# Two attentions on one core: third key tile padded from 16 to 128 rows, three score products in one PSUM bank

## The chip, the cores and the metric

The kernel runs on one core of a Trainium2 chip. The metric is device time in microseconds (us) of one execution; lower is better. The engines named here are PE (TensorE, matrix products; PEld is its weight load), DVE (VectorE), ACT (ScalarE), POOL (GpSimd) and SP (the queue that starts the loads from HBM).

## What is computed

The reference chains two transformer blocks over 256 tokens with 16 meta tokens in front (width 1024, float32). The first block (convolution mixers and a layer of 16384 small experts) is not touched by the change. The second block runs two attentions side by side on the normed input, eight heads each:

```
def stick_breaking_block(q, k, v, qpos, kpos):
    z = einsum('bhqd,bhkd->bhqk', q, k) * (SB_HEAD_DIM ** -0.5)
    causal = kpos[None, :] < qpos[:, None]
    u = where(causal, log_sigmoid(-z), 0.0)
    rest = cumsum(u, axis=3, reverse=True) - u
    a = where(causal, exp(log_sigmoid(z) + rest), 0.0)
    return einsum('bhqk,bhkd->bhqd', a, v)

def diff_attn_block(q, k, v, lam, slopes, qpos, kpos, qcid, kcid):
    s = einsum('bhcqd,bhckd->bhcqk', q, k) * (DF_HEAD_DIM ** -0.5)
    s = where(kcid <= qcid, s - slopes * abs(qpos - kpos), -inf)
    p = softmax(s)
    w = p[:, :, 0] - lam * p[:, :, 1]
    return einsum('bhqk,bhkd->bhqd', w, v)
```

The keys are 272 (16 + 256), so over tiles of 128 they are two whole tiles and one of 16. The queries are the 256 tokens.

## The kernel before, in words

Weights come in units of 128x1024 float32: SP loads a unit (`load_to`, L124), ACT and DVE split it into a rounded part and a rest (`split_to`, L145; the split is made two units ahead), and PE multiplies rounded and rest parts in `mm_w` (L164 to 171): 24 matmuls for each unit, with 256 or 272 columns moving. PE's and SP's order is the order of the program text; the order of ACT, DVE and POOL is set by a scheduler.

In the second block each head of an attention takes three units (query, key and value projections, `feat`, L871). Between the units PE does the small products of the heads that are under way; each head is a Python generator (`stick`, L892; `diff`, L930), and `advance` (L996) lets every running head do its next piece after each unit.

A stick-breaking head does this, with keys on the partitions and queries along the columns. For each of the three key tiles (`KT`, L839: 128, 128 and 16 keys; the queries that can see them are 256, 144 and 16, `Q0`, L840) it makes a product z of key and query (L897), each in a PSUM bank of its own (`at_tile`, L73, four banks in turn). DVE adds the causal mask (L899), ACT and DVE form the softplus e (L901 to 904). Two pieces later, PE sums e along the keys by products with a triangle or with ones (L917, product S, six of them, two or four touching the 16 rows), DVE subtracts (L918), ACT exponentiates (L919). Two pieces later the value product po (L924) adds up over the three tiles. `value` (L883) transposes the values by PE before that (pv_sv, pv_dv). A differential head makes its scores with 64 rows of key and query (ds, L941), turns the weights by PE transposes (pw, L963) and multiplies them by the values (dpo, L972: for the first 128 queries one tile of 128 keys and one of 16, for the second two of 128 and one of 16).

These small products are plain float32, of which PE runs each matmul as two instructions ("passes" in the following), with a weight load for each; transposes are one pass. The trace writes a matmul's weights as rows*columns: `16*128` is a weight tile of 16 rows and 128 columns.

The lines that the change touches are these:

```
839     KT = [(0, P), (P, P), (2 * P, NM)]
...
897             nc.tensor.matmul(pz[:kn, :n], k[:, k0:k0 + kn], q[:, Q0[kt]:], start=True, stop=True)
...
917                 nc.tensor.matmul(ps[:kn, Q0[j] - Q0[kt]:n], w[:jn, :kn], sps[j][:jn], start=(j == kt), stop=(j == 2))
...
924             nc.tensor.matmul(po[:, Q0[kt]:T], vt[:kn, kt, :], zs[kt][:kn], start=(kt == 0), stop=(kt == 2))
...
963                 nc.tensor.transpose(pw[:n, i * P:(i + 1) * P], ws[t][:, k0:k0 + n], ident)
...
972                 nc.tensor.matmul(po[:, :P], wT[:n, i, :], vt[:n, i, :], start=(i == 0), stop=(i == tl[-1][0]))
```

Of the kernel before, what the change touches and what calls it, by code (L numbers as in the profile page):

```python
# [8 lines left out]
F32 = mybir.dt.float32  # L9
# [41 lines left out]
def two_blocks(ctx, tc, x, feats, vecs, w_in, w_out, w_q, keys, u, v, final_g, meta2, w_in2, lams, w_gate,  # L51
# [787 lines left out]
    KT = [(0, P), (P, P), (2 * P, NM)]  # L839
    Q0 = [0, 112, 240]  # L840
    QS = slice(NM, L)
# [7 lines left out]
    mneg = []  # L849
    for kt, (k0, kn) in enumerate(KT):  # L850
        m = psb.tile([P, T - Q0[kt]], F32, tag=f"mneg{kt}", name=f"mneg{kt}")
        nc.gpsimd.memset(m, 0.0)
        nc.gpsimd.affine_select(m[:kn], m[:kn], [[1, T - Q0[kt]]], ALU.is_gt, -BIG, base=NM + Q0[kt] - k0,
                                channel_multiplier=-1)
        mneg.append(m)
# [15 lines left out]
    def feat(name, tag, cols, scale=1.0):  # L871
        width = cols.stop - cols.start
        ps = mm_tile(f"ps_{name}")
        mm_w(ps[:, :width], xT2, cols)

        def scaled():
            o = psb.tile([P, width], F32, tag=tag, name=name, bufs=2)
            nc.vector.scalar_tensor_tensor(o, ps[:, :width], scale, rsb[:, cols], op0=ALU.mult, op1=ALU.mult)
            return o

        return scaled

    def value(name, tag, vt):  # L883
        ps = at_tile(f"pv_{name}")
        o = psb.tile([P, 3, P], F32, tag=tag, name=name, bufs=2)
        for kt, (k0, kn) in enumerate(KT):
            nc.tensor.transpose(ps[:kn, kt * P:(kt + 1) * P], vt[:, k0:k0 + kn], ident)
        nc.scalar.activation(o[:, :2, :], ps[:, :2 * P].rearrange("p (a b) -> p a b", a=2), AF.Copy)
        nc.scalar.activation(o[:NM, 2, :], ps[:NM, 2 * P:3 * P], AF.Copy)
        return o  # L890

    def stick(hd, q, k, vT):  # L892
        zs, sps = [], []
        for kt, (k0, kn) in enumerate(KT):
            n = T - Q0[kt]
            pz = at_tile(f"z{hd}{kt}")
            nc.tensor.matmul(pz[:kn, :n], k[:, k0:k0 + kn], q[:, Q0[kt]:], start=True, stop=True)  # L897
            z = psb.tile([P, n], F32, tag=f"z{kt}", name=f"zs{hd}{kt}", bufs=2)
            nc.vector.tensor_tensor(z[:kn], pz[:kn, :n], mneg[kt][:kn], op=ALU.add)  # L899
            e = psb.tile([P, n], F32, tag=f"e{kt}", name=f"e{hd}{kt}", bufs=2)  # L900
            nc.scalar.activation(e[:kn], z[:kn], AF.Abs)  # L901
            nc.scalar.activation(e[:kn], e[:kn], AF.Exp, scale=-1.0)
            nc.scalar.activation(e[:kn], e[:kn], AF.Ln, bias=1.0)
            nc.vector.scalar_tensor_tensor(e[:kn], z[:kn], 0.0, e[:kn], op0=ALU.max, op1=ALU.add)
            zs.append(z)
            sps.append(e)
# [4 lines left out]
        for kt, (k0, kn) in enumerate(KT):  # L911
            n = T - Q0[kt]
            ps = at_tile(f"S{hd}{kt}")
            for j in range(kt, 3):
                jn = KT[j][1]
                w = tri if j == kt else ones
                nc.tensor.matmul(ps[:kn, Q0[j] - Q0[kt]:n], w[:jn, :kn], sps[j][:jn], start=(j == kt), stop=(j == 2))  # L917
            nc.vector.tensor_tensor(zs[kt][:kn], zs[kt][:kn], ps[:kn, :n], op=ALU.subtract)  # L918
            nc.scalar.activation(zs[kt][:kn], zs[kt][:kn], AF.Exp)  # L919
# [3 lines left out]
        for kt, (k0, kn) in enumerate(KT):  # L923
            nc.tensor.matmul(po[:, Q0[kt]:T], vt[:kn, kt, :], zs[kt][:kn], start=(kt == 0), stop=(kt == 2))  # L924
# [5 lines left out]
    def diff(hd, q, k, vT):  # L930
        slope = 2.0 ** (-(hd + 1))
        ws = []
        for t in range(2):
# [15 lines left out]
            nc.vector.scalar_tensor_tensor(pe[0], pe[0], sm[:, 0:1], pe[1], op0=ALU.mult, op1=ALU.subtract)  # L949
            ws.append(pe[0])  # L950
# [6 lines left out]
        for t in range(2):  # L957
            kn = KN[t]
            pw = at_tile(f"pw{hd}{t}")
            wT = psb.tile([P, 3, P], F32, tag="wT", name=f"wT{hd}{t}", bufs=2)  # L960
            tl = [(i, k0, min(n, kn - k0)) for i, (k0, n) in enumerate(KT) if k0 < kn]
            for i, k0, n in tl:
                nc.tensor.transpose(pw[:n, i * P:(i + 1) * P], ws[t][:, k0:k0 + n], ident)  # L963
            f = len(tl) - 1
            nc.scalar.activation(wT[:, :f, :], pw[:, :f * P].rearrange("p (a b) -> p a b", a=f), AF.Copy)
            nc.scalar.activation(wT[:NM, f, :], pw[:NM, f * P:(f + 1) * P], AF.Copy)
            outs.append((wT, tl))
        yield
        for t, (wT, tl) in enumerate(outs):
            po = at_tile(f"dpo{hd}{t}")  # L970
            for i, k0, n in tl:
                nc.tensor.matmul(po[:, :P], wT[:n, i, :], vt[:n, i, :], start=(i == 0), stop=(i == tl[-1][0]))  # L972
            nc.scalar.activation(od[t][:, hd, :], po[:, :P], AF.Copy)
# [27 lines left out]
    for hd in range(NH):  # L1001
        q = feat(f"sq{hd}", "sq", QS, float(P) ** -0.5)
# [3 lines left out]
        k = feat(f"sk{hd}", "sk", FULL)  # L1006
# [6 lines left out]
        vT = feat(f"svT{hd}", "vT", FULL)  # L1013
# [11 lines left out]
    for hd in range(NH):  # L1025
        q = feat(f"dq{hd}", "dq", QS, 0.125)()
        advance()
        k = feat(f"dk{hd}", "dk", FULL)()
        advance()
        vT = feat(f"dvT{hd}", "vT", FULL)()  # L1030
# [162 lines left out]
```

## Time and profile before

| | before |
|---|---|
| time, median of 3 runs (us) | 1479.19 (1478.61, 1479.19, 1486.41) |
| time of the profiled execution (us) | 1478.11 |
| its span, first to last instruction (us) | 1476.4 |
| mean granted TensorE clock | 0.997 |
| busy: PE, PEld, DVE, ACT, POOL (us) | 1446.7, 1338.5, 1059.0, 746.6, 14.1 |
| DMA, mean (GB/s) | 169 |

Starts and durations below are us from the start of the span. A matmul's recorded duration overlaps that of its neighbours, so what a matmul costs is read from the distance between starts, not from the duration. The two attentions stand between about 950 and 1177 us: stick-breaking heads to about 1070, differential heads after.

### The profile page before, as it was taken

The page shows a single profiled execution, that of the slowest core. Times are in us where ns is not written, and L with a number is a line of the kernel's source. Part 1 is how long each engine was busy: PE and PEld are TensorE (multiplying, and loading weights), DVE is VectorE, ACT ScalarE, POOL GpSimd, SP SyncE. Part 2 cuts the span into 40 slices and gives each one's busy share as a digit, 9 for nine tenths or more (in the row PEclk, how much of TensorE's full clock was granted, in tenths as well). Part 3 has the DMA queues.
Part 4 walks back from the last instruction along what each step waited for, and adds up shares of the span by engine and source line. Part 5 has one row for each costly group of instructions (what it writes and reads, how often), then busy time and mean ns, then how long its engine had stood idle before and what let it go on. Part 6 is the DMA issues. An engine that isn't in the chain of part 4 may idle for free.

```text
span 1476.4 us, 25739 instructions
## 1 busy us (share of the span) xinstructions
PE 1446.7 (98%) x10096; PEld 1338.5 (91%) x10096; DVE 1059.0 (72%) x1936; ACT 746.6 (51%) x1312; POOL 14.1 (1%) x32
## 2 busy tenths in 40 slices
PE   8999999999999999999999999999999999999998
PEld 7988999999999999788888888889998999899997
DVE  8987669779788999655555565755577776766665
ACT  7556444445444443344444445655455674554444
POOL 0010000000000000000000000100000000000000
PEclk9999999999999999999999999999999999999999
DMA  7626666665544444466666676633334456556662
GB/s 236 199 72 201 197 177 193 189 184 186 168 140 143 143 144 129 141 192 195 188 196 196 191 252 190 190 125 115 127 115 130 128 171 184 165 186 194 187 187 98
DMA packets 69816, 248.96 MB, mean 169 GB/s; under 512 B 7744, under 2 KB 9152, under 8 KB 69696
## 3 DMA queue, kind: packets, MB, share of 16 engines
q1 hardware_dynamic: 68544, 243.13, 52.9%
q0 software_dynamic: 1152, 4.19, 0.8%
q8 instruction: 79, 1.29, 0.4%
q14 instruction: 41, 0.34, 0.1%
HBM read 245.20 MB, written 2.10 MB: 168 GB/s over the span
## 4 chain that ended last, share of the span: by engine, by line
PE 93%; DVE 5%; issue 1%; DMA 0%; ACT 0%; SPq 0%; DVEq 0%; ACTq 0%
PE v L184 8%; PE v L182 8%; PE v L183 8%; PE u L171 7%; PE u L169 7%; PE u L170 7%; PE gp L675 4%; PE fg L170 1%; PE fu L171 1%; PE fg L171 1%; PE fu L170 1%; PE fd L184 1%; PE fu L169 1%; PE fg L169 1%; PE fd L183 1%; PE fd L182 1%
## 5 line engine op out<-in xcount | busy, mean ns | idle before, releaser
L152 DVE TENSOR_TENSOR lo<-raw,hi 128x1024 fp32r<-128x1024 f32 x453 | 552.9, 1223 | 241.4 <-ACT hi L150 239.9
L150 ACT ACTIVATE hi<-raw 128x1024 fp32r<-128x1024 f32 x453 | 478.6, 1058 | 469.7 <-PE u L170 122.7
L169 PE MATMUL u<-hThi,hi 128*128 128x256 f32 x1024 | 289.9, 283 | 0.0
L171 PE MATMUL u<-hThi,lo 128*128 128x256 f32 x1024 | 285.3, 279 | 0.1
L170 PE MATMUL u<-hTlo,hi 128*128 128x256 f32 x1024 | 284.9, 278 | 0.0
L182 PE MATMUL v<-hi,w_hi 128*128 128x512 f32 x512 | 199.3, 389 | 1.3 <-ACT w_hi L764 1.3
L184 PE MATMUL v<-hi,w_lo 128*128 128x512 f32 x512 | 199.3, 389 | 0.5 <-DVE w_lo L766 0.5
L183 PE MATMUL v<-lo,w_hi 128*128 128x512 f32 x512 | 199.2, 389 | 0.0
L170 PEld LDWEIGHTS u<-hTlo,hi 128*128 128x128 f32 x1024 | 194.0, 189 | 0.0
L171 PEld LDWEIGHTS u<-hThi,lo 128*128 128x128 f32 x1024 | 192.3, 188 | 0.8 <-DVE lo L152 0.7
L169 PEld LDWEIGHTS u<-hThi,hi 128*128 128x128 f32 x1024 | 192.5, 188 | 0.0
L182 PEld LDWEIGHTS v<-hi,w_hi 128*128 128x128 f32 x512 | 96.1, 188 | 21.4 <-ACT w_hi L764 1.5
L184 PEld LDWEIGHTS v<-hi,w_lo 128*128 128x128 f32 x512 | 96.1, 188 | 20.9 <-DVE w_lo L766 1.0
L183 PEld LDWEIGHTS v<-lo,w_hi 128*128 128x128 f32 x512 | 96.1, 188 | 20.1 <-DVE lo L152 0.2
L675 PE MATMUL gp<-ga,gb 128*128 128x128 f32 x512 | 66.6, 275 | 4.0 <-DVE gb L666 4.0
L764 ACT ACTIVATE w_hi<-ewa 128x512 fp32r<-128x512 f32 x48 | 30.2, 632 | 76.7 <-PE v L183 65.9
L675 PEld LDWEIGHTS gp<-ga,gb 128*128 128x128 f32 x512 | 61.7, 191 | 4.8 <-PE gp L675 3.6
L766 DVE TENSOR_TENSOR w_lo<-ewa,w_hi 128x512 fp32r<-128x512 f32 x48 | 33.2, 693 | 38.6 <-ACT w_hi L764 38.6
L662 DVE TENSOR_TENSOR ga<-o,o 128x512 f32<-128x512 f32 x64 | 44.0, 687 | 17.8 <-PE gp L675 17.3
L170 PE MATMUL fg<-hTlo,hi 128*128 128x256 f32 x176 | 49.2, 280 | 0.5 <-DVE hTlo L223 0.5
L169 PE MATMUL fg<-hThi,hi 128*128 128x256 f32 x176 | 49.3, 280 | 0.3 <-ACT hThi L222 0.3
L171 PE MATMUL fu<-hThi,lo 128*128 128x256 f32 x176 | 49.1, 279 | 0.0
(403 smaller groups left out, 2970.6 us busy)
## 6 DMA issues: line engine op xcount, KB each, us to landing
raw<-in_u_dram SPq DMA_DIRECT2D x128, 512.0 KB, 3.6
raw<-in_v_dram SPq DMA_DIRECT2D x128, 512.0 KB, 3.6
raw<-in_w_in_dram SPq DMA_DIRECT2D x67, 512.0 KB, 3.6
raw<-in_w_fg_dram SPq DMA_DIRECT2D x22, 512.0 KB, 3.6
raw<-in_w_fu_dram SPq DMA_DIRECT2D x22, 512.0 KB, 3.6
raw<-in_w_fd_dram SPq DMA_DIRECT2D x22, 512.0 KB, 3.6
raw<-in_w_out_dram SPq DMA_DIRECT2D x16, 512.0 KB, 3.6
raw<-in_w_q_dram SPq DMA_DIRECT2D x16, 512.0 KB, 4.3
```

The costliest lines, as they stand in the source:

```text
L150: latest["hi"] = nc.scalar.activation(hi, loaded[i], AF.Copy)
L152: latest["lo"] = nc.vector.tensor_tensor(lo, loaded[i], hi.bitcast(F32), op=ALU.subtract)
L169: nc.tensor.matmul(ps, hi[:, ks], ahi[:, k, cols], start=(k == 0), stop=False)
L170: nc.tensor.matmul(ps, hi[:, ks], alo[:, k, cols], start=False, stop=False)
L171: nc.tensor.matmul(ps, lo[:, ks], ahi[:, k, cols], start=False, stop=(k == KC - 1))
L182: nc.tensor.matmul(ps, ahi[:, ts], hi[:, bs], start=first and n == 0, stop=False)
L183: nc.tensor.matmul(ps, ahi[:, ts], lo[:, bs], start=False, stop=False)
L184: nc.tensor.matmul(ps, alo[:, ts], hi[:, bs], start=False, stop=end)
L662: nc.vector.tensor_tensor(a.rearrange("p t (h l) -> p t h l", h=8), o8[:, tl, :].unsqueeze(3).broadcast_to((P, 4, 8, TOPK)), o16[:, tl, :] ...
L675: nc.tensor.matmul(p3[:, :, i], b[:, i, :], a[:, i, :], start=True, stop=True)
L764: nc.scalar.activation(hi, a, AF.Copy)
L766: nc.vector.tensor_tensor(lo, a, hi.bitcast(F32), op=ALU.subtract)
```

## The change: padding, one bank, and fewer instructions off PE

The key and value tiles become 384 columns wide and the differential weights 256 and 384, with zeros in the columns past the 272 keys (or past 144 for the first 128 queries); the zeros are written once by POOL into buffers that stay (two for the keys, one for the values, one for each of the two weight tiles). Every product over the third key tile then has 128 rows and 128 weight columns. The three z of a stick-breaking head stand side by side in one bank (256 + 144 + 16 = 416 columns), and so do its three S; DVE and ACT handle them with one instruction of 416 columns in place of three.

```
-    KT = [(0, P), (P, P), (2 * P, NM)]
+    KP = 3 * P
     Q0 = [0, 112, 240]
+    QN = [T - q0 for q0 in Q0]
+    QO = [0, QN[0], QN[0] + QN[1]]
+    NQ = sum(QN)
...
+    KW = [2 * P, KP]
+    padded = {}
+    for tag, n, w in (("k", L, KP), ("vT", L, KP), ("w0", KN[0], KW[0]), ("w1", KN[1], KW[1])):
+        padded[tag] = [psb.tile([P, w], F32, tag=f"{tag}{i}", name=f"{tag}pad{i}")
+                       for i in range(2 if tag == "k" else 1)]
+        for o in padded[tag]:
+            nc.gpsimd.memset(o[:, n:], 0.0)
...
+    def qcols(kt, j=None):
+        j = kt if j is None else j
+        return slice(QO[kt] + Q0[j] - Q0[kt], QO[kt] + QN[kt])
+
     def stick(hd, q, k, vT):
...
+        pz = at_tile(f"z{hd}")
+        for kt in range(3):
+            nc.tensor.matmul(pz[:, qcols(kt)], k[:, kt * P:(kt + 1) * P], q[:, Q0[kt]:], start=True, stop=True)
+        z = psb.tile([P, NQ], F32, tag="z", name=f"zs{hd}", bufs=2)
+        nc.vector.tensor_tensor(z, pz[:, :NQ], mneg, op=ALU.add)
+        e = psb.tile([P, NQ], F32, tag="e", name=f"e{hd}", bufs=2)
+        nc.scalar.activation(e, z, AF.Abs)
+        nc.scalar.activation(e, e, AF.Exp, scale=-1.0)
+        nc.scalar.activation(e, e, AF.Ln, bias=1.0)
+        nc.vector.scalar_tensor_tensor(e, z, 0.0, e, op0=ALU.max, op1=ALU.add)
...
+        ps = at_tile(f"S{hd}")
+        for kt in range(3):
             for j in range(kt, 3):
...
+                nc.tensor.matmul(ps[:, qcols(kt, j)], tri if j == kt else ones, e[:, qcols(j)],
+                                 start=(j == kt), stop=(j == 2))
+        nc.vector.tensor_tensor(z, z, ps[:, :NQ], op=ALU.subtract)
+        nc.scalar.activation(z, z, AF.Exp)
...
+        for kt in range(3):
+            nc.tensor.matmul(po[:, Q0[kt]:T], vt[:, kt, :], z[:, qcols(kt)], start=(kt == 0), stop=(kt == 2))
...
+            for i in range(nk):
+                nc.tensor.transpose(pw[:, i * P:(i + 1) * P], ws[t][:, i * P:(i + 1) * P], ident)
...
+            for i in range(nk):
+                nc.tensor.matmul(po[:, :P], wT[:, i, :], vt[:, i, :], start=(i == 0), stop=(i == nk - 1))
```

PE, the pieces S and z between two projections of a stick-breaking head, before (tiles are out<-in; the last number pair is the output's rows x columns):

```order
L917 MATMUL S_10796<-e_10661,tri 128x256
L917 MATMUL S_10796<-e_10670,ones 128x144
L917 MATMUL S_10796<-e_10679,ones 128x16
L917 MATMUL S_10802<-e_10670,tri 128x144
L917 MATMUL S_10802<-e_10679,ones 128x16
L917 MATMUL S_10807<-e_10679,tri 16x16
L897 MATMUL z_10811<-sq_10715,sk_10755 128x256
L897 MATMUL z_10820<-sq_10715,sk_10755 128x144
L897 MATMUL z_10829<-sq_10715,sk_10755 16x16
```

The same place in the change:

```order
L924 MATMUL S_10706<-e_10592,tri 128x256
L924 MATMUL S_10706<-e_10592,ones 128x144
L924 MATMUL S_10706<-e_10592,ones 128x16
L924 MATMUL S_10706<-e_10592,tri 128x144
L924 MATMUL S_10706<-e_10592,ones 128x16
L924 MATMUL S_10706<-e_10592,tri 128x16
L909 MATMUL z_10715<-sq_10628,kpad_10049 128x256
L909 MATMUL z_10715<-sq_10628,kpad_10049 128x144
L909 MATMUL z_10715<-sq_10628,kpad_10049 128x16
```

Nothing moved and the count is the same; the outputs of 16 rows became 128 rows, and S and z are one tile each.

DVE, from the value projection's scaling to the next query's, before (lo is the rest part of a weight unit, zs the masked z, e the softplus):

```order
L878 SCALAR_TENSOR_TENSOR svT_10794<-ps_svT_10763,rsb 128x272
L918 TENSOR_TENSOR zs_10659<-zs_10659,S_10796 128x256
L918 TENSOR_TENSOR zs_10668<-zs_10668,S_10802 128x144
L918 TENSOR_TENSOR zs_10677<-zs_10677,S_10807 16x16
L899 TENSOR_TENSOR zs_10813<-z_10811,mneg_10032 128x256
L899 TENSOR_TENSOR zs_10822<-z_10820,mneg_10037 128x144
L899 TENSOR_TENSOR zs_10831<-z_10829,mneg_10042 16x16
L152 TENSOR_TENSOR lo_10843<-raw_10725,hi_10841 128x1024
L904 SCALAR_TENSOR_TENSOR e_10815<-zs_10813,e_10815 128x256
L904 SCALAR_TENSOR_TENSOR e_10824<-zs_10822,e_10824 128x144
L904 SCALAR_TENSOR_TENSOR e_10833<-zs_10831,e_10833 16x16
```

The same place in the change:

```order
L889 SCALAR_TENSOR_TENSOR vTpad_10053<-ps_svT_10674,rsb 128x272
L152 TENSOR_TENSOR lo_10731<-raw_10637,hi_10729 128x1024
L926 TENSOR_TENSOR zs_10590<-zs_10590,S_10706 128x416
L911 TENSOR_TENSOR zs_10719<-z_10715,mneg 128x416
L889 SCALAR_TENSOR_TENSOR sq_10757<-ps_sq_10726,rsb 128x256
L916 SCALAR_TENSOR_TENSOR e_10721<-zs_10719,e_10721 128x416
```

Nine instructions became three, the weight split lo now stands ahead of the two that wait for S and z, and the next query's scaling (sq) ahead of the last step of e.

## Rows read from the trace of the kernel before

**Rows 1.** The page: PE's busy time and the chain that ended last, by engine.

```profile
PE 1446.7 (98%) x10096; PEld 1338.5 (91%) x10096; DVE 1059.0 (72%) x1936; ACT 746.6 (51%) x1312; POOL 14.1 (1%) x32
...
PE 93%; DVE 5%; issue 1%; DMA 0%; ACT 0%; SPq 0%; DVEq 0%; ACTq 0%
```

**Rows 2.** Busy time in the stretch of one differential head: length, PE, PEld, DVE, ACT, POOL.

```profile
1108.30:1121.20 12.90, 12.90 (x100) 11.64 (x98) 9.19 (x21) 6.93 (x20) 0.00 (x0) 1.00 0.41 123
```

**Rows 3.** PE in order of time, S and z of a stick-breaking head: start, us, instructions.

```profile
1000.54 0.59 PE L917 MATMUL S<-e,tri 128*128 128x256 f32 x2
...
1002.07 0.39 PE L917 MATMUL S<-e,ones 16*128 16x16 f32 x2
...
1002.53 1.09 PE L897 MATMUL z<-sq,sk 128*128 128x256 f32 x6
1003.55 0.39 PE L169 MATMUL ps_sq<-xT2hi,hi 128*128 128x256 f32 x1
1003.78 0.28 PE L170 MATMUL ps_sq<-xT2lo,hi 128*128 128x256 f32 x1
1003.90 0.28 PE L171 MATMUL ps_sq<-xT2hi,lo 128*128 128x256 f32 x1
```

**Rows 4.** PE in order of time, po of a stick-breaking head.

```profile
996.32 1.16 PE L924 MATMUL po<-zs,sv 128*128 128x256 f32 x6
997.41 0.40 PE L169 MATMUL ps_svT<-xT2hi,hi 128*128 128x272 f32 x1
```

**Rows 5.** PE in order of time, dpo of a differential head, whole and piece by piece.

```profile
1137.49 1.85 PE L972 MATMUL dpo<-dv,wT 128*128 128x128 f32 x10
1139.27 0.50 PE L941 MATMUL ds<-dk,dq 64*128 64x272 f32 x2
...
1137.80 0.48 PE L972 MATMUL dpo<-dv,wT 16*128 16x128 f32 x2
...
1138.22 0.38 PE L972 MATMUL dpo<-dv,wT 128*128 128x128 f32 x1
```

**Rows 6.** PE in order of time: eight float32 passes of full weights, 128 columns moving.

```profile
162.06 1.06 PE L539 MATMUL sc<-kt,qT 128*128 128x128 f32 x8
162.87 0.37 PE L169 MATMUL u<-hThi,hi 128*128 128x256 f32 x1
163.07 0.28 PE L170 MATMUL u<-hTlo,hi 128*128 128x256 f32 x1
```

**Rows 7.** PE in order of time: full weights with 16 columns moving, then 256 columns.

```profile
89.35 0.29 PE L250 MATMUL m_s<-m_q,ones 128*128 128x16 f32 x2
89.49 0.48 PE L182 MATMUL wo<-hi,yhi 128*128 128x512 f32 x1
89.81 0.39 PE L183 MATMUL wo<-lo,yhi 128*128 128x512 f32 x1
90.04 0.40 PE L184 MATMUL wo<-hi,ylo 128*128 128x512 f32 x1
...
98.19 0.59 PE L425 MATMUL ln_var<-csq,inv 128*128 128x256 f32 x2
98.62 0.50 PE L463 MATMUL pss<-ones,ysq 128*128 128x1 f32 x4
```

**Rows 8.** PE in order of time: the three value transposes, the third of 16 weight columns.

```profile
1006.49 0.49 PE L887 MATMUL pv_sv<-ident,svT 128*128 128x128 f32 x3
1006.73 0.38 PE L169 MATMUL ps_sk<-xT2hi,hi 128*128 128x272 f32 x1
1006.95 0.29 PE L170 MATMUL ps_sk<-xT2lo,hi 128*128 128x272 f32 x1
```

**Rows 9.** DVE's last step of e, and the S product that reads it.

```profile
1006.03 0.16 DVE L904 SCALAR_TENSOR_TENSOR e<-zs,e 16x16 f32<-16x16 f32 x1 [0.17 <-ACT e L903]
...
1014.07 0.38 PE L917 MATMUL S<-e,tri 128*128 128x256 f32 x1
```

**Rows 10.** Busy time by stretch ahead of the first head; the seventh field is PEclk.

```profile
962.70:966.20 3.50, 3.50 (x19) 3.50 (x19) 0.86 (x3) 1.03 (x2) 0.00 (x0) 0.51 0.44 174
```

More of the change, by code (lines that the diff above doesn't have):

```diff
@@ L846, in two_blocks @@
     s_sb, psb = phase("psb")
[L849 to L855, printed above, removed]
+    mneg = psb.tile([P, NQ], F32, tag="mneg", name="mneg")
+    nc.gpsimd.memset(mneg, 0.0)
+    for kt in range(3):
+        o = mneg[:, QO[kt]:QO[kt] + QN[kt]]
+        nc.gpsimd.affine_select(o, o, [[1, QN[kt]]], ALU.is_gt, -BIG, base=NM + Q0[kt] - kt * P, channel_multiplier=-1)
     tri = psb.tile([P, P], F32, tag="tri", name="tri")
@@ L876, in scaled @@
         def scaled():
-            o = psb.tile([P, width], F32, tag=tag, name=name, bufs=2)
-            nc.vector.scalar_tensor_tensor(o, ps[:, :width], scale, rsb[:, cols], op0=ALU.mult, op1=ALU.mult)
+            o = padded[tag][hd % len(padded[tag])] if tag in padded else psb.tile([P, width], F32, tag=tag, name=name, bufs=2)
+            nc.vector.scalar_tensor_tensor(o[:, :width], ps[:, :width], scale, rsb[:, cols], op0=ALU.mult, op1=ALU.mult)
             return o
@@ L885, in value @@
         o = psb.tile([P, 3, P], F32, tag=tag, name=name, bufs=2)
[L886 to L889, printed above, removed]
-        return o
+        for kt in range(3):
+            nc.tensor.transpose(ps[:, kt * P:(kt + 1) * P], vt[:, kt * P:(kt + 1) * P], ident)
+        nc.scalar.activation(o, ps[:, :KP].rearrange("p (a b) -> p a b", a=3), AF.Copy)
+        return o
+    def qcols(kt, j=None):
+        j = kt if j is None else j
+        return slice(QO[kt] + Q0[j] - Q0[kt], QO[kt] + QN[kt])
     def stick(hd, q, k, vT):
[L893 to L906, printed above, removed]
+        pz = at_tile(f"z{hd}")
[8 more added lines that the diff above has]
+        nc.vector.scalar_tensor_tensor(e, z, 0.0, e, op0=ALU.max, op1=ALU.add)
         yield
@@ L910, in stick @@
         yield
-        for kt, (k0, kn) in enumerate(KT):
-            n = T - Q0[kt]
-            ps = at_tile(f"S{hd}{kt}")
+        ps = at_tile(f"S{hd}")
+        for kt in range(3):
             for j in range(kt, 3):
[L915 to L919, printed above, removed]
+                nc.tensor.matmul(ps[:, qcols(kt, j)], tri if j == kt else ones, e[:, qcols(j)],
+                                 start=(j == kt), stop=(j == 2))
+        nc.vector.tensor_tensor(z, z, ps[:, :NQ], op=ALU.subtract)
+        nc.scalar.activation(z, z, AF.Exp)
         yield
@@ L922, in stick @@
         po = at_tile(f"po{hd}")
-        for kt, (k0, kn) in enumerate(KT):
-            nc.tensor.matmul(po[:, Q0[kt]:T], vt[:kn, kt, :], zs[kt][:kn], start=(kt == 0), stop=(kt == 2))
+        for kt in range(3):
+            nc.tensor.matmul(po[:, Q0[kt]:T], vt[:, kt, :], z[:, qcols(kt)], start=(kt == 0), stop=(kt == 2))
         nc.scalar.activation(osb[0][:, hd, :], po[:, :T], AF.Copy)
@@ L948, in diff @@
             nc.vector.tensor_scalar(pe[1], pe[1], sm[:, 1:2], lam, op0=ALU.mult, op1=ALU.mult)
-            nc.vector.scalar_tensor_tensor(pe[0], pe[0], sm[:, 0:1], pe[1], op0=ALU.mult, op1=ALU.subtract)
-            ws.append(pe[0])
+            w = padded[f"w{t}"][0]
+            nc.vector.scalar_tensor_tensor(w[:, :kn], pe[0], sm[:, 0:1], pe[1], op0=ALU.mult, op1=ALU.subtract)
+            ws.append(w)
             if t == 0:
@@ L1025, in two_blocks @@
     for hd in range(NH):
-        q = feat(f"dq{hd}", "dq", QS, 0.125)()
+        q = feat(f"dq{hd}", hd, "dq", QS, 0.125)()
         advance()
-        k = feat(f"dk{hd}", "dk", FULL)()
+        k = feat(f"dk{hd}", hd, "k", FULL)()
         advance()
-        vT = feat(f"dvT{hd}", "vT", FULL)()
+        vT = feat(f"dvT{hd}", hd, "vT", FULL)()
         running.append(diff(hd, q, k, vT))
```

24 lines of the change are left out of this document (9 added, 15 removed).

## The prediction

> **What bounds the kernel.** I read the page first: PE is busy 98% of the span and is 93% of the chain that ended last [rows 1]. Then the stretch of one differential head, the denser kind for DVE: PE is busy for all of its 12.90 us, DVE for 9.19 and ACT for 6.93 [rows 2]. So around the change PE is the bound, and only what changes PE's own time, or makes PE wait, changes the result. Then PE in order of time, by distances between starts, since recorded durations overlap.
>
> There the products over the 16-key tile stand out. In dpo the two passes of 16 rows start at 1137.80 and the next product at 1138.22: 0.21 us for each pass of 128 columns [rows 5]. Eight float32 passes of the same 128 columns with full 128-row weights take, with one wide product behind them, 163.07 - 162.06 = 1.01 us; less 0.12 for that product, 0.111 each [rows 6]. So a 16-row pass costs almost twice a full one, though it does an eighth of the work. The two full passes ahead of it are late as well: 1137.49 to 1137.80 is 0.31 where two should take 0.22 [rows 5]. And the first wide product after a block that ended in the 16-key tile is followed by the next one after 0.23 us, when the pace is 0.12 [rows 3]. I read this as a fixed loss, some 0.1 us, each time PE changes between full weights and weights of 16 rows or 16 columns, in both directions. The change removes these shapes, except the 64-row scores ds.
>
> **Prices of passes with full weights.** 256 columns: (98.62 - 98.19) / 2 = 0.215 us [rows 7]. 128 columns: 0.111 [rows 6]. 144 columns: no such row stands free of a change of shape; a straight line between these two gives 0.124. 16 columns, the padded third tile: m_s is the same shape, two passes and then wide products; 89.35 to 89.81 is 0.46, less 0.23 for one wide product (89.81 to 90.04) leaves 0.23, so 0.115 each [rows 7]. That is nearly the price of 128 columns: such a pass waits for its own weight load. The lower end for it is 0.07, half the distance from m_s to the next start (0.14) [rows 7]; the upper end is the 0.21 of a 16-row pass in dpo [rows 5]. I take 0.115, because that row has the same shape and the same full neighbours.
>
> **The sum, block by block.**
> - S and z of a stick-breaking head, 18 passes. Before: 1000.54 to 1003.78, less the 0.12 of one normal step, is 3.12 us [rows 3]. After: four passes of 256, six of 144, eight of 16 columns: 0.86 + 0.74 + 0.92 = 2.52. Gain 0.60.
> - po, six passes. Before: 996.32 to 997.41 is 1.09 [rows 4], and the late next product adds the 0.11 of rows 3: 1.20. After: 0.43 + 0.25 + 0.23 = 0.91. Gain 0.29.
> - Over eight heads 8 x 0.89 = 7.1; in the first two heads and the last S and z do not stand together, so I take 7.0.
> - dpo, ten passes. Before: 1137.49 to 1139.27 is 1.78 [rows 5]. After: nine of 0.111, and a last one that is still followed by a change of shape, to the 64-row ds, at the 0.21 that a pass next to a change has now: 1.21. Gain 0.57, times eight heads 4.6.
> - The transposes (pv, pw): the third, with 16 weight columns, already costs a whole one. 1006.49 to 1006.95 is 0.46, less one step of 0.13 (0.12 scaled to 272 columns) is 0.33, three times 0.11 [rows 8]. Padding changes nothing: 0.
> - DVE and ACT lose about half the instructions of a stick-breaking head; POOL gets five small fills behind work that is done before the first head. The engines have idle time beside PE [rows 2]: 0. If PE stopped covering them, this would count as a gain, not a loss.
> - Waits. e is complete at 1006.03 + 0.16 = 1006.19, and the S that reads it starts at 1014.07 [rows 9]: 7.9 us in hand. One bank means that DVE starts its subtraction only when the whole S is there, but S is over sooner, and three short instructions become one. The weight split lo moves ahead of that wait, which is safer for PE. The single buffer for the values is read by the transposes two projections before it is written again. I cost these at 0.
>
> Together 7.0 + 4.6 = 11.6 us. The sum is made against the profiled execution: 1478.11 - 11.6 = **1466.5 us**. That execution stands 1.1 us under the median of the runs shown, so the change against the median would be 12.7. A bound of another kind: PE's clock was granted at 0.51 in a stretch of 3.5 us ahead of the first head [rows 10], which at full speed would be 1.7 us shorter; the stretch can fall otherwise in the new kernel.
>
> **A rule that speaks against it.** A 16-row pass costs 0.21 us and a full one 0.111 [rows 5, 6]. The Trainium skill (TensorE: Matmul & The Clock Gate, section "Why this matters for your kernels") says that one matmul with a contraction of 32 takes the same time as one of 128, and that small contractions gain only by running side by side. By that rule the padding gains nothing; it is the rival "no gain" below. The rows disagree with it here, next to a change of shape. Of narrow passes the same page (section "Back-to-back issue gap") says that 1 to 64 columns take about 60 cycles, with a floor near 25 ns. By it, as an estimate, the 80 narrow passes would cost 0.09 us less each than I put, and the time would be 1459.3. The 0.115 of rows 7 contradicts it where every pass brings new weights.
>
> **Rivals.**
> - *Narrow passes are cheap.* With the lower end, 0.07, 80 passes (ten in each of eight heads) save 0.045 more each: 3.6 us, 1462.9. For it: the starts in m_s lie close [rows 7]. Against it: what follows them comes late by the difference. Chance 0.09.
> - *Narrow passes are dear.* With the upper end, 0.21, they take back 80 x 0.095 = 7.6 us and only dpo's part and little else is left: 1474.1. For it: they alternate with wide ones in S as now. Against it: rows 7. Chance 0.07.
> - *No gain.* The excess belongs to the third tile in the sum, not to its shape: dpo stays at 1.78, and four passes of a head that now load 16 weight columns load 128. At 0.05 each, about half of a narrow pass, 32 of them cost 1.6: 1479.7. Against it: the full products behind are late too [rows 3]. Chance 0.05.
> - *Slower: PE waits for e.* The place is S, through the DVE queue: the subtraction waits for all of S, and behind it stand the mask addition, the next query's scaling and the last step of e. It decides only once e comes later by the 7.9 us in hand [rows 9]; from there on every microsecond is PE's. With 3 us of wait in each of eight heads: 1466.5 + 24 = 1490.5. Against it: the margin, and a shorter chain. Chance 0.04.
> - *The change does not do what it says*, because the scheduler reorders it: PE's order is the program's, and the rows of the order show full shapes there. I give it nothing of its own.
>
> **How the numbers follow.** The forecast, 1464 to 1469 with the clock's 1.7 us and the rounding of the starts, has 0.75. The range 1462.5 to 1470.5 holds it and nearly all of the cheap case. A measurement of this kernel can tell about 0.5%, 7.4 us, from no change: faster means under 1471.8. The forecast, the cheap case and less than half of the dear one lie there: 0.87. The rest of the dear case, no gain, and a small wait: 0.10. Slower: 0.03.
>
> **What would show it.** S and z together should take 2.5 us instead of 3.12, po 0.9, dpo 1.2, the first wide product after each should no longer be late by 0.1, and PE should be busy without gaps between 966 us and the end of the differential heads. The transposes should stay at 0.11 each. The prediction is wrong if m_s is no model for narrow passes in S (S over 1.75 us or under 1.4 where I sum 1.6), if dpo stays above 1.5, or if PE waits for DVE or ACT ahead of S, po or pw.

## The result and the profile after

The changed kernel takes 1469.85 us (median of four runs, 1468.40 to 1472.70); the kernel before took 1479.97 beside it. The ratio is 0.9933, with an interval of 0.9917 to 0.9949: 10.1 us faster. A second comparison gave 12.9 us (below). The forecast was 1466.5, the range 1462.5 to 1470.5.

The page still shows PE as the bound, with less work: 1440.7 us instead of the 1446.7 of [rows 1]. The page of the kernel after, busy time and chain:

```profile
PE 1440.7 (98%) x10096; PEld 1341.6 (91%) x10096; DVE 1052.5 (72%) x1888; ACT 737.6 (50%) x1216; POOL 14.7 (1%) x35
...
PE 94%; DVE 3%; DMA 1%; issue 1%; ACT 0%; SPq 0%; POOL 0%; DVEq 0%; ACTq 0%
```

PE executes as many instructions as before (10096): padding added none. DVE has 48 fewer and ACT 96 fewer; neither was the bound. The stretch of one differential head, the answer to [rows 2], is full of PE as before and 0.58 us shorter (windows of the kernel after; columns as in rows 2):

```profile
1109.62:1121.94 12.32, 12.32 (x101) 11.53 (x99) 9.02 (x21) 6.76 (x16) 0.00 (x0) 1.00 0.38 128
```

PE in order of time in the kernel after (start, us, instruction): the start of both attentions, S and z of a stick-breaking head [rows 3], its output po [rows 4], the S of the next head, the transposes and scores of a differential head, its output dpo [rows 5], and the end of both attentions.

```profile
972.59 0.60 PE L909 MATMUL z<-sq,kpad 128*128 128x256 f32 x2
...
1017.60 0.59 PE L924 MATMUL S<-e,tri 128*128 128x256 f32 x2
...
1018.41 0.49 PE L924 MATMUL S<-e,tri 128*128 128x144 f32 x2
1018.74 0.29 PE L924 MATMUL S<-e,ones 128*128 128x16 f32 x2
1018.88 0.37 PE L924 MATMUL S<-e,tri 128*128 128x16 f32 x2
1019.10 1.05 PE L909 MATMUL z<-sq,kpad 128*128 128x256 f32 x6
1020.00 0.37 PE L169 MATMUL ps_sq<-xT2hi,hi 128*128 128x256 f32 x1
1020.21 0.28 PE L170 MATMUL ps_sq<-xT2lo,hi 128*128 128x256 f32 x1
...
1026.26 0.97 PE L932 MATMUL po<-zs,sv 128*128 128x256 f32 x6
1027.07 0.37 PE L169 MATMUL ps_svT<-xT2hi,hi 128*128 128x272 f32 x1
1027.28 0.29 PE L170 MATMUL ps_svT<-xT2lo,hi 128*128 128x272 f32 x1
...
1030.18 0.59 PE L924 MATMUL S<-e,tri 128*128 128x256 f32 x2
...
1117.93 0.38 PE L971 MATMUL pw<-ident,w0pad 128*128 128x128 f32 x2
...
1118.57 0.52 PE L949 MATMUL ds<-kpad,dq 64*128 64x144 f32 x4
1119.02 0.39 PE L169 MATMUL ps_dq<-xT2hi,hi 128*128 128x256 f32 x1
1119.24 0.28 PE L170 MATMUL ps_dq<-xT2lo,hi 128*128 128x256 f32 x1
...
1121.94 1.28 PE L979 MATMUL dpo<-dv,wT 128*128 128x128 f32 x10
1123.14 0.73 PE L949 MATMUL ds<-kpad,dq 64*128 64x272 f32 x4
...
1185.42 0.82 PE L995 MATMUL dtr<-ident,od 128*128 128x128 f32 x6
```

From start to start, S takes 1.50 us where it took 1.99 [rows 3], po 0.81 (1.09 in rows 4), dpo 1.20 (1.78 in rows 5). The first row starts both attentions; the last one (dtr, the transposes of the differential heads' outputs) stands 14 us behind the last dpo, the same in both kernels. From the one to the other it is 1185.42 - 972.59 = 212.83 us. The same two instructions of the kernel before, from its PE in order of time:

```profile
966.15 0.60 PE L897 MATMUL z<-sq,sk 128*128 128x256 f32 x2
...
1191.19 0.60 PE L988 MATMUL dtr<-ident,od 128*128 128x128 f32 x4
```

That is 225.04 us. **The attentions are 12.2 us shorter**, 2 us more than the first medians differ. But they begin 6.4 us later (972.59 instead of 966.15), in a part of the program that the change does not touch. Part of that is TensorE's granted clock, which was at its lower level (1.2 GHz, half) longer than in the kernel before. Windows of the kernel after; the seventh field is the clock:

```profile
122.50:129.50 7.00, 6.10 (x28) 5.72 (x29) 5.45 (x8) 3.49 (x5) 0.00 (x0) 0.51 0.10 29
...
600.40:607.30 6.90, 6.38 (x16) 4.81 (x16) 1.69 (x4) 1.06 (x1) 0.00 (x0) 0.51 0.27 76
...
969.00:972.60 3.60, 3.60 (x20) 3.60 (x20) 0.95 (x3) 1.10 (x1) 0.00 (x0) 0.53 0.50 160
```

The kernel before had only the last of these, a few us earlier [rows 10]. How much each costs is read from the same instruction in both traces: across the first stretch PE's lag behind the kernel before grows by 2.1 us (0.28 to 2.41), across the second by 2.8 (3.22 to 6.03). So these two make 4.9 of the 6.4 us. The other 1.5 arise at full clock: 0.24 at the first product, 0.8 between 200 and 400 us (after_again has these 0.8 too), 0.35 near 860. In every profile below the clock is at its upper level from the first z to dtr, so these stretches do not touch the length of the attentions.

### The profile page after: what moved, and what is told of

It is laid out like the page before. It is cut to its first block, busy times and chain, and to the rows that moved or that the text cites. A ratio compares the mean times of both kernels' runs of the same rounds, so it can differ in the third digit from the quotient of the medians.

```text
span 1470.5 us, 25555 instructions
## 1 busy us (share of the span) xinstructions
PE 1440.7 (98%) x10096; PEld 1341.6 (91%) x10096; DVE 1052.5 (72%) x1888; ACT 737.6 (50%) x1216; POOL 14.7 (1%) x35
## 4 chain that ended last, share of the span: by engine, by line
PE 94%; DVE 3%; DMA 1%; issue 1%; ACT 0%; SPq 0%; POOL 0%; DVEq 0%; ACTq 0%
PE u L171 8%; PE u L169 8%; PE u L170 8%; PE v L184 8%; PE v L183 8%; PE v L182 8%; PE gp L675 4%; PE fg L170 1%; PE fu L171 1%; PE fg L171 1%; PE fd L184 1%; PE fu L170 1%; PE fu L169 1%; PE fg L169 1%; PE fd L183 1%; PE fd L182 1%
```

## The experiments

The theory is the prediction's: each time PE goes from weights of 128 rows to the 16-row third tile and back, it loses a fixed time, and full weights everywhere remove this. The rivals: the weight columns are the cause and not the rows; or the shared bank and the merged DVE and ACT steps earn the gain; or the change brings the half-clock stretches and so costs something outside. The table has each block from start to start (us, medians over the heads), the length of both attentions (first z to dtr), and the median beside that of the kernel before in the same comparison.

| kernel | S | z | po | dpo | attentions | median | before | runs |
|---|---|---|---|---|---|---|---|---|
| before | 1.992 | 1.019 | 1.089 | 1.780 | 225.04 | | 1479.97 | 4 |
| after | 1.508 | .900 | .816 | 1.207 | 212.84 | 1469.85 | 1479.97 | 4 |
| after_again | 1.508 | .900 | .816 | 1.207 | 212.83 | 1467.70 | 1480.59 | 5 |
| diff_only | 1.992 | 1.018 | 1.089 | 1.207 | 220.22 | 1476.87 | 1480.59 | 10 |
| stick_only | 1.508 | .900 | .816 | 1.782 | 217.68 | 1472.65 | 1480.59 | 4 |
| three_banks | 1.509 | .900 | .816 | 1.207 | 213.21 | 1469.97 | 1480.59 | 4 |
| short_rows | 2.076 | .921 | 1.089 | 1.783 | 224.70 | 1481.05 | 1479.79 | 1 |
| narrow_weights | 1.510 | 1.019 | .816 | 1.207 | 214.38 | 1470.36 | 1479.79 | 1 |
| wide_third | 1.508 | .900 | .816 | 1.208 | 212.87 | 1467.88 | 1479.79 | 1 |
| merged_ones | 1.285 | .900 | .816 | 1.207 | 211.17 | 1468.69 | 1479.79 | 4 |
| full_scores | 1.508 | .900 | .816 | 1.207 | 211.71 | 1471.25 | 1480.13 | 1 |
| both_more | 1.285 | .900 | .816 | 1.207 | 210.06 | 1466.59 | 1480.13 | 6 |
| both_more_again | 1.285 | .900 | .816 | 1.207 | 210.04 | 1465.87 | 1480.17 | 5 |
| before_again | 1.992 | 1.018 | 1.089 | 1.780 | 225.05 | 1485.97 | 1480.13 | 1 |

Where there is one run, its time stands for the median. The attentions' length repeats to 0.02 us between executions of one kernel, while single runs scatter by several us. So the table's column of lengths decides between theories, and the medians only confirm.

**after_again**: the changed kernel, unedited.

> The changed kernel once more. In its profile the two attentions gained 12.1 us (S with z 3.01 to 2.41, po 1.09 to 0.82, dpo 1.78 to 1.21, as starts), yet the medians differ by 10.1 only. Theory A: the missing 2 us are stretches of half clock that fall by chance outside the attentions, at PE's waits; then the attentions again gain 12.1 in the trace, the half-clock stretches stand elsewhere or are fewer, and over five rounds the time comes out 10 to 12 us under the kernel before, the runs with the higher mean clock being the faster ones. Theory B: the change itself costs 2 us outside the attentions; then the same loss stands at the same place again, at any clock.

1467.70 (1467.22 to 1469.65), ratio 0.9918 with 0.9905 to 0.9932: 12.9 us faster. The attentions again gained 12.2, and the profiled execution, between its first 15 us and its last 10, had one half-clock stretch only, of 3.4 us near 598. The missing 2 us of the first comparison lay outside the attentions.

**diff_only**: only the padding of the differential heads; the stick-breaking heads as before.

```diff
-        pz = at_tile(f"z{hd}")
-        for kt in range(3):
-            nc.tensor.matmul(pz[:, qcols(kt)], k[:, kt * P:(kt + 1) * P], q[:, Q0[kt]:], start=True, stop=True)
...
+        for kt, (k0, kn) in enumerate(KT):
+            n = T - Q0[kt]
+            pz = at_tile(f"z{hd}{kt}")
+            nc.tensor.matmul(pz[:kn, :n], k[:, k0:k0 + kn], q[:, Q0[kt]:], start=True, stop=True)
...
-            nc.tensor.matmul(po[:, Q0[kt]:T], vt[:, kt, :], z[:, qcols(kt)], start=(kt == 0), stop=(kt == 2))
+        for kt, (k0, kn) in enumerate(KT):
+            nc.tensor.matmul(po[:, Q0[kt]:T], vt[:kn, kt, :], zs[kt][:kn], start=(kt == 0), stop=(kt == 2))
```

> Padding in the differential heads alone; the stick-breaking products keep three banks and their 16-row third tile. Theory of shapes: dpo 1.21 us in the trace, S 1.99, z 1.02, po 1.09 as before; 4.7 us faster than before. Rival, that the excess belongs to something other than the shape (semaphores, the order in the sum): dpo stays near 1.8 and the time within 1 us of before.

1476.87, ratio 0.9973 with 0.9964 to 0.9982. The attentions are 4.8 us shorter, all of it in dpo.

**stick_only**: the other half; the differential heads as before.

```diff
...
-            for i in range(nk):
-                nc.tensor.matmul(po[:, :P], wT[:, i, :], vt[:, i, :], start=(i == 0), stop=(i == nk - 1))
+            for i, k0, n in tl:
+                nc.tensor.matmul(po[:, :P], wT[:n, i, :], vt[:n, i, :], start=(i == 0), stop=(i == tl[-1][0]))
```

> Padding and shared bank in the stick-breaking heads alone; the differential weights keep their 16-row tile. Theory of shapes: S 1.51 us, z 0.90, po 0.82 in the trace, dpo 1.78 as before; 7.4 us faster than before, and together with the differential heads alone it adds up to the whole. Rival, that the two parts hold each other up: the sum of the two differs from the whole by more than 1.5 us in the trace.

1472.65, ratio 0.9945 with 0.9929 to 0.9960. The attentions are 7.4 us shorter. 7.4 and 4.8 make the 12.2 of the whole: the halves add up, and neither triggers anything in the other.

**three_banks**: every shape padded as in the change, but z and S of each key tile in a bank of its own, with DVE and ACT steps for each tile, as before.

```diff
-        pz = at_tile(f"z{hd}")
...
         for kt in range(3):
-            nc.tensor.matmul(pz[:, qcols(kt)], k[:, kt * P:(kt + 1) * P], q[:, Q0[kt]:], start=True, stop=True)
...
+            n = QN[kt]
+            pz = at_tile(f"z{hd}{kt}")
+            nc.tensor.matmul(pz[:, :n], k[:, kt * P:(kt + 1) * P], q[:, Q0[kt]:], start=True, stop=True)
...
```

> The padding everywhere, but each of the three z and S of a stick-breaking head in a bank of its own again, with three instructions on DVE and ACT where the change has one. Theory of shapes: PE is the bound, so S 1.5, z 0.9, po 0.82 and dpo 1.21 as in the change, and the time within 1 us of it. Rival, that the shared bank and the fewer instructions bring part of the gain: PE waits or slower blocks, 2 us or more slower than the change.

1469.97, ratio 0.9923 with 0.9908 to 0.9938, blocks as in the change. The attentions are 0.37 us longer than the change's, all of it at one place: in the third head z comes late, because it waits for DVE to finish with an output tile (osblo, L938), whose bank z is to take (PE in order of time):

```profile
991.34 1.07 PE L911 MATMUL z<-sq,kpad 128*128 128x256 f32 x6 [0.22 <-DVE osblo L938]
```

The kernel before, with as many banks in use, has no such wait. So the shared bank is worth at most 0.4 of the 12.2 us: the rival falls.

**short_rows**: the change with 16-row contractions of the third tile in S, po and dpo, and nothing else.

```diff
...
-            nc.tensor.matmul(po[:, Q0[kt]:T], vt[:, kt, :], z[:, qcols(kt)], start=(kt == 0), stop=(kt == 2))
+            jn = P if kt < 2 else NM
+            nc.tensor.matmul(po[:, Q0[kt]:T], vt[:jn, kt, :], z[:jn, qcols(kt)], start=(kt == 0), stop=(kt == 2))
...
```

> The change, with the third tile's products of S, the stick output and the differential output contracted over its 16 filled rows again instead of 128 padded ones; their weights keep all 128 columns, and nothing else differs. What is missing are only products with zero rows. If the change's gain comes from the contraction's rows (a pass of 16 rows has to wait for the passes of 128 rows and they for it), the differential outputs go back from 1.21 to about 1.78 us a head, the stick output from .82 to about 1.09, S from 1.51 to between 1.85 and 2.0, z stays at .90, and the time is about 8 x (.57 + .27 + .4) = 10 us above the change, near 1478. If the rows do not matter and the gain came from the full columns of the weights (16 columns before in S and z), all four blocks stay as in the change and the time is near 1468.

1481.05: the gain is gone. S and dpo in this kernel's PE order, beside the change's above:

```profile
1018.07 0.51 PE L925 MATMUL S<-e,tri 128*128 128x144 f32 x2
1018.52 0.39 PE L925 MATMUL S<-e,ones 16*128 16x16 f32 x2
...
1019.06 1.07 PE L909 MATMUL z<-sq,kpad 128*128 128x256 f32 x6
...
1114.56 1.85 PE L982 MATMUL dpo<-dv,wT 128*128 128x128 f32 x10
1116.34 0.73 PE L951 MATMUL ds<-kpad,dq 64*128 64x272 f32 x4
```

From the product before to the first 16-row one it is 0.45 us (1018.07 to 1018.52); with full rows it is 0.33 (1018.41 to 1018.74). The blocks give one price. S goes to the 16-row shape and back twice and lost 2.076 - 1.508 = 0.57, and z behind it 0.02; dpo goes twice, 0.58; po once, 0.27 and 0.02 in its follower. **An excursion into 16 rows and back costs 0.29 us**, over two passes or four, with 16 columns moving or 128. Counted by passes the price would not be one: 0.10 for each of the six 16-row passes of S, 0.14 to 0.15 in dpo and po.

The attentions lost 11.9 us where 10 was expected. S came out above the expected 1.85 to 2.0, and above the 1.99 of the kernel before, because there its last product has 16 weight columns as well as 16 rows: the last two products take 0.46 us (1002.07 to 1002.53 [rows 3]) and here 0.54 (1018.52 to 1019.06).

The weight loads in order of time show where the loss begins: the load for the first 16-row product in short_rows, then the load for the same product with full rows in the change.

```profile
1018.51 0.29 PEld L925 LDWEIGHTS S<-e,ones 16*128 16x128 f32 x2
...
1018.62 0.31 PEld L924 LDWEIGHTS S<-e,ones 128*128 128x128 f32 x2
```

With full rows the load starts 0.12 us ahead of its product (1018.62, 1018.74), beside the product that still runs. With 16 rows it starts together with its product (1018.51, 1018.52): at the change of rows nothing is loaded ahead. The load itself takes no longer with 16 rows (0.29 us for the two passes, 0.31 with 128). The Trainium skill (TensorEngine Tiling (Array Packing), section "Key Properties") says that a change of tiling mode, not only of the tile, drains TensorE. The trace agrees in that the cost goes with the change and not with the passes; a drain as such no run shows.

**narrow_weights**: the counterpart: 128 rows everywhere, but 16 weight columns (16 output rows) for the third tile of z and S; three banks.

```diff
...
-            nc.tensor.matmul(pz[:, qcols(kt)], k[:, kt * P:(kt + 1) * P], q[:, Q0[kt]:], start=True, stop=True)
...
+            kn = P if kt < 2 else NM
...
+            nc.tensor.matmul(pz[:kn, :n], k[:, kt * P:kt * P + kn], q[:, Q0[kt]:], start=True, stop=True)
...
+                nc.tensor.matmul(ps[:kn, Q0[j] - Q0[kt]:n], (tri if j == kt else ones)[:, :kn], sps[j], start=(j == kt), stop=(j == 2))
...
```

> The change, with the third tile of z and of S computed for its 16 keys alone again (weights of 16 columns, an output of 16 partitions), while every contraction keeps 128 rows; z and S take three banks, as in the kernel before. Here only the columns of the weights go back. If the rows are the cause and the columns matter only for themselves, the stick output stays at .82 us and the differential outputs at 1.21, z goes back to about 1.02 (it has no other difference to the kernel before), and S, where one product of six now has 16 columns of weights, lies between 1.4 and 1.65; the time is 0 to 2 us above the change. If the columns are the cause of S's gain, S goes to 1.85 us or more and the time is 3 us or more above the change.

S stays at 1.510 and po and dpo as in the change: rows are the cause there. z goes back to 1.019. The attentions are 1.17 us longer than in three_banks, which has full weights and the same wait for a bank. PE's order:

```profile
1016.06 0.29 PE L935 MATMUL S<-ethird,ones 128*128 128x16 f32 x2
1016.28 0.21 PE L935 MATMUL S<-ethird,tri 128*16 128x16 f32 x2
1016.42 1.09 PE L916 MATMUL z<-sq,kpad 128*128 128x256 f32 x6
1017.44 0.39 PE L169 MATMUL ps_sq<-xT2hi,hi 128*128 128x256 f32 x1
1017.67 0.28 PE L170 MATMUL ps_sq<-xT2lo,hi 128*128 128x256 f32 x1
```

The product of 16 weight columns starts 0.22 us after the narrow product before it (1016.06 to 1016.28) where the change needs 0.14, and then is through in 0.14 where the change needs 0.22: the switch costs 0.08, and the shorter weight loads give it back. In z, where the third product stands alone behind wide ones, only the cost is left: 0.12 us, and 0.02 in the follower.

**wide_third**: z's third product moves 96 columns instead of 16.

```diff
-            nc.tensor.matmul(pz[:, qcols(kt)], k[:, kt * P:(kt + 1) * P], q[:, Q0[kt]:], start=True, stop=True)
+            rhs, dst = q[:, Q0[kt]:], pz[:, qcols(kt)]
+            if kt == 2:
+                rhs = rhs.unsqueeze(1).broadcast_to((P, 6, NM))
+                dst = pz[:, QO[2]:QO[2] + 6 * NM].rearrange("p (a b) -> p a b", a=6)
+            nc.tensor.matmul(dst, k[:, kt * P:(kt + 1) * P], rhs, start=True, stop=True)
```

> The change, with z's third product moving 96 columns (its 16, six times over) into columns of the bank that nothing reads. If a narrow pass over new weights costs what it takes to load the weights (.11 us a pass in the prediction's pricing, 8 passes in z's three products... the third has two or four of them by the number's halves), its 16 or 96 columns make no difference: z stays at .90 us a head and the time within .5 us of the change. If a pass is paid by the columns that it moves, 80 more columns in each pass of the third product cost .033 us a pass or more (128 columns take about .11 in the same records, so 80 about .07), .13 or more a head: z goes to 1.03 or more, and the time 1 us or more up.

z stays at 0.900 us, the attentions at 212.87: six times the columns cost nothing. So what a narrow pass costs here is not its columns; that it is the weight load, as the row m_s [rows 7] had suggested, fits narrow_weights, where fewer weight columns made it shorter.

**merged_ones**: the change, with the two products of S that share weights and moving data made as one.

```diff
-        for kt in range(3):
-            for j in range(kt, 3):
-                nc.tensor.matmul(ps[:, qcols(kt, j)], tri if j == kt else ones, e[:, qcols(j)],
-                                 start=(j == kt), stop=(j == 2))
+        nc.tensor.matmul(ps[:, qcols(0)], tri, e[:, qcols(0)], start=True, stop=False)
+        nc.tensor.matmul(ps[:, qcols(0, 1)], ones, e[:, qcols(1)], start=False, stop=False)
+        nc.tensor.matmul(ps[:, qcols(1)], tri, e[:, qcols(1)], start=False, stop=False)
+        both = ps[:, Q0[1]:QO[2]].rearrange("p (a b) -> p a b", a=2)[:, :, QN[1] - NM:]
+        nc.tensor.matmul(both, ones, e[:, qcols(2)].unsqueeze(1).broadcast_to((P, 2, NM)), start=False, stop=False)
+        nc.tensor.matmul(ps[:, qcols(2)], tri, e[:, qcols(2)], start=False, stop=True)
```

> The change, with the two products of S that have the same weights (ones) and the same moving data (the third tile's 16 columns of e) made as one product of 32 columns, which writes both places of the shared bank through a strided output; only the first product of the bank clears. It needs the shared bank of the change. If a narrow pass costs its weight load, the two or more passes saved per head are worth .11 us each: the narrow product has 4 passes at full precision as z's, so S falls from 1.51 to between 1.1 and 1.3 us a head, and the time by 1.8 to 3.5 us. If narrow passes are nearly free once no shape changes (some .025 us each), S falls by .05 to .1 and the time by less than 1 us.

```profile
1016.00 0.59 PE L922 MATMUL S<-e,tri 128*128 128x256 f32 x2
...
1016.93 0.30 PE L926 MATMUL S<-e,ones 128*128 128x32 f32 x2
1017.07 0.38 PE L927 MATMUL S<-e,tri 128*128 128x16 f32 x2
1017.29 1.05 PE L909 MATMUL z<-sq,kpad 128*128 128x256 f32 x6
```

A product is two passes in the records, not four as the expectation's "or more" allowed for, so two passes are saved: S falls by 0.223, 0.112 each, and the attentions by 1.67 us, a little under the 1.8 to 3.5 expected. The median, 11.1 us under the kernel before, lies between the change's 10.1 and 12.9 and does not show it. The prediction's 0.115 for a narrow pass is measured here by itself.

**full_scores**: the change, with the scores of the first 128 queries of a differential head contracted over 128 rows instead of 64; the other half of the rows is zero. The differential values also take the buffers of the stick-breaking ones (`sv`).

```diff
...
+        for c in range(2):
+            nc.gpsimd.tensor_copy(halves_q[c][hd % 2][64 * c:64 * c + 64], q[64 * c:64 * c + 64, :P])
...
-                nc.tensor.matmul(ps[:, :kn], q[cs, t * P:(t + 1) * P], k[cs, :kn], start=True, stop=True)
+                if t == 0:
+                    nc.tensor.matmul(ps[:, :kn], halves_q[c][hd % 2], k[:, :kn], start=True, stop=True)
+                else:
+                    nc.tensor.matmul(ps[:, :kn], q[cs, t * P:(t + 1) * P], k[cs, :kn], start=True, stop=True)
...
-        vt = value(f"dv{hd}", "dv", vT)
+        vt = value(f"dv{hd}", "sv", vT)
```

> The change with the second of these edits alone: 128-row products for the first 128 queries of the differential scores. If the 64-row shape costs a wait at each change, as the 16-row one does, the transposes ahead of the scores go from .637 to about .545 us, and the product behind the scores is no longer late: .14 us a head and 1.1 us in all, near 1467. If not, the blocks keep their times. If TensorE comes to wait for GpSimd's copies, the scores' block grows and a wait on POOL stands in the profile.

```profile
1117.62 0.38 PE L981 MATMUL pw<-ident,w0pad 128*128 128x128 f32 x2
...
1118.17 0.66 PE L957 MATMUL ds<-kpad,qhalf 128*128 128x144 f32 x4
1118.57 0.37 PE L169 MATMUL ps_dq<-xT2hi,hi 128*128 128x256 f32 x1
1118.78 0.28 PE L170 MATMUL ps_dq<-xT2lo,hi 128*128 128x256 f32 x1
```

The transposes go from 0.64 us (1117.93 to 1118.57 in the change) to 0.55, and from the scores' start to the second product of the projection it is 0.61 instead of 0.67. That is 0.15 us a head; the attentions are 1.13 shorter, as expected. The single run's 1471.25 had 6.8 us of half clock near 122, and more elsewhere.

**both_more** and **both_more_again**: the last two edits together.

> The change with two further edits. First, the merged product of S alone (the two products with ones and the third tile's columns in one of 32 columns), which took .22 us a head off S where it ran by itself: 1.8 us. Second, the four 64-row score products of each differential head that serve the first 128 queries contract over 128 rows instead (each half of the queries stands in a 128-row tile whose other half is zero, copied by GpSimd). If a change between 64 and 128 rows costs as the one between 16 and 128 does, the transposes and scores of a differential head lose about .14 us, 1.1 us in all, and the time is 2.9 us under the change: 1464 to 1465.5 beside a change of 1468, S 1.285 a head. If changes of 64 rows cost nothing, or the copies make the scores late, only the 1.8 us remain: 1466 or more.

> The kernel with both further edits, unchanged, timed again: its first six runs lay between 1464.6 and 1473.0, too wide to set it against the change. By its blocks its two attentions are 2.9 us shorter than the change's; if that reaches the total, the median is near 1465 beside a kernel before of 1480, a difference of 15 us where the change's five longer-timed runs had 12.9. If the rest of the kernel gives it back, the difference is 13 us or less. The half-clock stretches outside the attentions (1.7 us each for 3.4 us of half clock) will again scatter single runs by some us.

1466.59 (1464.60 to 1473.01), ratio 0.9913 with 0.9894 to 0.9932; then 1465.87 (1464.35 to 1469.26), ratio 0.9912 with 0.9896 to 0.9928. The attentions are 2.8 us shorter than the change's in both profiles. The medians lie 13.5 and 14.3 us under the kernel before, where 15 was expected and the change had 10.1 and 12.9; the intervals overlap, so by the whole time alone this version is not shown to beat the change, only by the stretch.

**before_again**: the kernel before, unedited.

> The kernel before, unchanged, profiled again: it asks whether the half-clock stretches near 122 and 600 us, which the change's first profile has and the first profile of before has not, come from the change or from chance. If from chance, this profile of the kernel before has at least one stretch of half clock at a place where its first profile had none, or lacks the one at 962.7; if from the change, it has the one at 962.7 alone. Blocks as in the first profile: S 1.99, z 1.02, stick output 1.09, differential outputs 1.78.

1485.97, with four half-clock stretches (windows, columns as above):

```profile
597.90:601.40 3.50, 3.19 (x8) 2.04 (x8) 1.59 (x3) 0.24 (x1) 0.00 (x0) 0.52 0.46 150
864.20:867.70 3.50, 3.50 (x10) 2.74 (x9) 2.21 (x3) 0.00 (x0) 0.00 (x0) 0.51 0.85 282
956.10:959.80 3.70, 3.70 (x18) 3.70 (x19) 3.64 (x5) 1.51 (x2) 0.00 (x0) 0.54 0.60 179
970.00:973.50 3.50, 3.50 (x19) 3.50 (x18) 1.12 (x3) 1.52 (x2) 0.00 (x0) 0.51 0.57 224
```

Three of them its first profile did not have, one near 598 among them. Its attentions began at 974.01, later than the change's 972.59, and took 225.05 us. So these stretches come and go with the execution, and the last rival falls for those near 600; the one near 122 stood in five profiles of padded kernels, was missing in seven others, after_again's among them, and in both of before; whether padding has a part in it is not settled.

## Why the prediction was right

**S and z.** Predicted 2.52 us instead of 3.12. Measured, in the same way: 1017.60 to 1020.21 is 2.61, less one step of 0.12, 2.49. **po**: predicted 0.91; 1026.26 to 1027.28 is 1.02, less a step of 0.13, 0.89. **dpo**: predicted 1.21, measured 1.207, and short_rows shows that the 16 rows alone make the difference. None of the limits named (S over 1.75 or under 1.4, dpo over 1.5, a wait of PE) was passed; S by itself took 1.51 where the working has 1.6.

**The sum.** 12.2 us for 11.6. Stick-breaking 7.4 for 7.0: from the S of one head to the S of the next it is 12.58 us (1017.60 to 1030.18) where it was 13.53 (1000.54 in rows 3 to 1014.07 in rows 9), so a head gains 0.94 and not 0.89. The deduction of 0.1 for S and z that stand apart came out about right: the last S, with 64-row scores behind it, went from 1.99 to 1.59 only. Differential 4.8 for 4.6: the last head's dpo, which has no 64-row scores behind it, went from 1.78 to 1.03 us.

**The zeros.** The transposes stayed (pv of a stick-breaking head 0.25 us before and after). The list of PE's waits between the first z and dtr is empty in both kernels, so the 7.9 us in hand for e [rows 9] sufficed and the slower rival never came near. DVE's and ACT's saved instructions earned nothing beyond the 0.4 us at the one bank wait of three_banks.

**The time itself.** 1469.85 lies 3.4 us over the forecast, inside the range. The sum was set against an execution of 1478.11, 1.9 us under the median of the kernel before in this comparison; the other 1.5 is the gain of 10.1 against 11.6, where the attentions gave 0.6 more and the rest of the program took 2.1 back. That the total came so near the sum is in part luck: of such scatter the prediction had named one half-clock stretch of 3.5 us, at 1.7 us. The profiles here have none to four stretches, of 3.4 or 6.8 us; the one ahead of the first head cost 1.5 in the kernel before (its lead over after_again falls from 2.2 to 0.7 us there), and PE has a wait near 860 us that comes and goes as well (last section).

**What was wrong in it.** It read the late first wide product as PE's loss on the way back from the narrow shape, and said that it would vanish. It did not: 1020.00 to 1020.21 is 0.21 where it had been 0.23 [rows 3] and the pace is 0.12. It is the narrow pass's own price, which shows one start later; the pricing by m_s had that inside, so the sum was right for another reason. Rows 6 had said so: behind eight full passes, with no change of shape, the same step is 0.20 (162.87 to 163.07). It put the loss at some 0.1 us in each direction, where an excursion costs 0.29; the sum did not use that figure. And it put 16 rows and 16 columns together as one loss. narrow_weights and short_rows part them: without the columns' 1.2 us, all of them in z, 11.0 of the 12.2 are the rows'. (short_rows alone lost 11.9; 0.7 of it because the last product of its S has 128 weight columns.)

**The rule on small contractions.** 16 rows cost more than 128 here, by 0.29 us an excursion, so that the Trainium skill's statement (TensorE: Matmul & The Clock Gate, section "Why this matters for your kernels"), that one matmul with a contraction of 32 takes the time of one with 128, does not carry over to 16 rows between full passes; no run here has such a pass by itself. The measurement decides, and the rival built on that statement is out.

## What to carry to other kernels

Count how often TensorE's order goes from full weight rows to a short tile and back, not how many short passes there are: here each such excursion cost 0.29 us, and padding with zeros, which adds arithmetic but no instruction, removed it. Where PE is busy without gaps, as it was here, the distances between starts of a handful of rows gave the gain to 5%. Judge a change of under 1% by the length of the stretch that it touches, bounded by two instructions in both traces, and not by whole runs alone.

## What the runs showed of the hardware

The half-clock stretches had not been expected to matter this much. Near 600 us the same wait stands ahead in an execution that has the stretch and in one that has not. PE in order of time in the kernel before:

```profile
596.65 0.50 PE L182 MATMUL v<-hi,w_hi 128*128 128x512 f32 x1 [1.31 <-ACT w_hi L764]
...
599.90 0.39 PE L183 MATMUL v<-lo,w_hi 128*128 128x512 f32 x1
600.13 0.40 PE L184 MATMUL v<-hi,w_lo 128*128 128x512 f32 x1
```

and in the kernel after:

```profile
599.87 0.50 PE L182 MATMUL v<-hi,w_hi 128*128 128x512 f32 x1 [1.31 <-ACT w_hi L764]
...
603.86 0.63 PE L184 MATMUL v<-hi,w_lo 128*128 128x512 f32 x1
604.29 0.63 PE L182 MATMUL v<-hi,w_hi 128*128 128x512 f32 x1
```

Both waited 1.31 us for the same conversion by ACT; afterwards one product follows the other after 0.23 us in the one (599.90 to 600.13) and after 0.43 in the other (603.86 to 604.29), at a granted clock of 0.51. Which execution gets the stretch was not explained.

The clock is not the only thing that comes and goes. The profile of both_more has no half-clock stretch between 15 and 1458 us, yet near 860 it lost 2.7 us on the kernel before: PE waited 2.57 us for the rest part of a weight unit, which DVE made late because it had itself waited 4.65 us for a load from HBM (the gain of L794). In the kernel before DVE waited 1.85 us for the same load, and PE not at all. merged_ones, full_scores and before_again have that wait of PE too (1.6, 1.1 and 2.3 us).

A 64-row excursion of the scores costs less than one of 16 rows: 0.15 us over what 128 rows take, measured in full_scores.
